# Reciprocal roots of a decoder trunk: from Newton steps on VectorE to a power on GpSimd

## The chip, the cores and the metric

The kernel runs on one core of a Trainium2 chip. The metric is the time of one execution on the device, in microseconds; lower is better. The core has five engines that run their own queues of instructions in order and meet at semaphores: TensorE (PE in the profile; its weight loads are PEld), VectorE (DVE), ScalarE (ACT), GpSimd (POOL) and SyncE (SP), which here only issues DMAs.

## The reference

Two layers work on a sequence of 2048 tokens of width 1024 in float32: a gated DeltaNet layer (GDN: 8 heads, keys of 128, values of 256) and a gated linear attention layer (GLA: 4 heads, the same sizes). Each ends in `x <- LayerNorm(alpha*x + mixer(x))`. What matters here are the places where a reciprocal root stands:

```python
def l2norm(t):
    return t * lax.rsqrt(jnp.sum(t * t, -1, keepdims=True) + L2_EPS)      # L2_EPS = 1e-6

def gated_rmsnorm(o, w, gate):
    o = o * lax.rsqrt(jnp.mean(o * o, -1, keepdims=True) + RMS_EPS)       # RMS_EPS = 1e-6
    return o * w.astype(jnp.float32) * jax.nn.silu(gate.astype(jnp.float32))

def layer_norm(x, g, b):
    xf = x.astype(jnp.float32)
    mu = jnp.mean(xf, -1, keepdims=True)
    xc = xf - mu
    var = jnp.mean(xc * xc, -1, keepdims=True)
    y = xc * lax.rsqrt(var + LN_EPS) * g.astype(jnp.float32) + b.astype(jnp.float32)   # LN_EPS = 1e-5
    return y.astype(x.dtype)

def gdn_mixer(x, w_in, conv_w, a_log, dt_bias, norm_w, w_out):
    ...
    q = l2norm(qkv[..., :GDN_KEY].reshape(B, T, GDN_HEADS, GDN_DK).astype(f32))
    k = l2norm(qkv[..., GDN_KEY:2 * GDN_KEY].reshape(B, T, GDN_HEADS, GDN_DK).astype(f32))
    ...
    o = gated_delta_rule(q, k, v, g, beta)
    o = gated_rmsnorm(o, norm_w, gate)
    return o.reshape(B, T, GDN_VAL).astype(x.dtype) @ w_out
```

The delta rule's output `o` is linear in `q`, so the norm of `q` is one factor for each token and head. GLA normalises its output in the same way, but neither `q` nor `k`.

## The kernel before

**Tiling.** The sequence is cut into 4 groups of 512 tokens (`TG`), each of 4 chunks of 128 (`NC`). A unit of work is one head of one layer on one group: 32 GDN units and 16 GLA units, in the order of `PHASES` (GDN of groups 0 and 1, then the layers in turn). Matrix products are done as three products of a high and a low part (`mm3`); the weights are loaded as `wraw`, ScalarE casts them to `wh`, and GpSimd subtracts to get `wl`. Nine such pairs of buffers exist (`W_BUFS`), and three PSUM tiles `psg` take the products.

**Four threads.** For each unit, `gemms` makes the input projection (`psg`), the short convolution (`acc`, on VectorE) and the gates (`sg`); `preps` makes what depends on keys and queries; `chains` runs the recurrence over the 4 chunks (`psh`, state `S`) and gathers the gated outputs `og` and their sums of squares `ssq`; `outs` multiplies by the output weights into `pso` and adds to `y`. `pso` has one buffer. The threads are interleaved by `Plan`: it prices every instruction as it is emitted (`COST`: a fixed time, a time for each element, and 800 ns until another instruction can use the result) and emits the next step whose operands it believes ready. The order of emission is the order of urgency; each engine then gets its own queue. Waits on semaphores follow from the tiles.

**The roots.** `rsqrt` works on VectorE: two operations on the bits make a first guess and nine operations (three steps of three) refine it. It is called in three places.

- In `gdn_prep`, once a unit: ScalarE squares the transposed keys and queries and accumulates their sums in `ss` (8 columns: 4 chunks of `k`, 4 of `q`); after the root `rr`, VectorE forms `rqs` (the root for `q`, scaled by 128 to the power of -0.5), `brk`, `br2` and `s1`. The products of keys (`D<-psc,br,D`) need `br2`. From there the preparation goes on: `W`, `X`, a transfer `blk` to memory and back as `Arep`, an inversion in 30 short steps of VectorE (`Xt`, `X`), and the matrices for `chains`. GpSimd takes part with a copy of `id16` into the buffer of `X`, which must wait until the transfer out of `X` has read it.
- In `chains`, once a unit: from `ssq` (and `rqs` for GDN) comes `z`, the factor for each token with which `outs` adds the product: `y <- pso * z + y`.
- In `layer_norm`, once for each chunk of 128 tokens of each layer, 32 times: `lnva` to `lnrs` and `lnmr`, which ScalarE then applies to `y`; VectorE multiplies by the gain, GpSimd adds the offset (VectorE in the very last chunk), and SyncE stores.

`load_wo` loads the output weights as `woraw`, and multiplies them by the norm's weight `nw` when it splits them (`woh` on ScalarE, `wol` on VectorE).

All engine operations but the DMAs' landings stand at one line of the profile, L121, since `Planned` issues them there; groups are told apart by their tiles. `z` is written by several operations, `ms`, `ztmp` beside it; `rr` goes with `rtmp`, `lnrs` with `lntmp`.

## Time and profile before

| what | value |
|---|---|
| median of 3 runs | 3253.21 us (3250.49 to 3254.4) |
| span of the profiled execution, first to last instruction | 3246.0 us |
| instructions | 55989 |
| traffic with memory | 91 GB/s over the span |

The profiled execution has no time of its own beside its span; the runs' median lies 7.2 us above it. The times in the profile are those of one execution. In the groups of instructions a line gives engine, operation, `out<-in` by the program's names, shapes and the count, then the busy time in us and the mean of one in ns, then the idle time of the engine just before them and what ended it. A line of waits gives who waited for whom, the total in us, how often, and the longest. A line of the timeline gives start and duration in us; `x4` are four in a row, and brackets hold the idle time before and its cause.

### The profile page before, as it was taken

What the parts mean: (1) busy time and instruction counts of PE and PEld (TensorE: products, weight loads), DVE (VectorE), ACT (ScalarE), POOL (GpSimd) and SP (SyncE); (2) the same over time, 40 slices, a digit from 0 to 9 for tenths busy, and PEclk for the clock granted to TensorE, in tenths of its full rate; (3) what the DMA queues carried; (4) which work ended last, traced back from release to release, by engine and by line L of the source; (5) the groups of instructions that cost most, each with busy time, mean ns of one, the idle gap of its engine ahead of it and who ended that gap; (6) DMA issues with size and microseconds to landing.
All of it is one profiled execution on the core that took longest, in us unless ns stands there. A gap on an engine that the chain in (4) does not pass through costs nothing.

```text
span 3246.0 us, 55989 instructions
## 1 busy us (share of the span) xinstructions
PE 3064.1 (94%) x18430; PEld 2601.6 (80%) x18430; DVE 2466.0 (76%) x6345; ACT 1565.6 (48%) x4099; POOL 1127.2 (35%) x1506
## 2 busy tenths in 40 slices
PE   8899999989999999998999999999899999899997
PEld 7688778768888888877887888978778878798885
DVE  7677788787877687688778768677877786866677
ACT  5445444445444456444444545553444454465542
POOL 5333333333233234334233324432433322433341
PEclk9899999999999999999999999999999999999998
DMA  6222223242222315324222322532422232243231
GB/s 179 63 77 74 78 73 98 82 147 76 74 78 78 101 53 153 109 79 127 80 79 82 92 73 67 153 98 78 136 77 74 82 94 69 78 137 97 66 125 59
DMA packets 311604, 299.83 MB, mean 92 GB/s; under 512 B 40544, under 2 KB 253792, under 8 KB 311312
## 3 DMA queue, kind: packets, MB, share of 16 engines
q1 hardware_dynamic: 285200, 278.42, 30.0%
q10 hardware_dynamic: 26112, 17.83, 1.9%
q8 instruction: 145, 2.38, 0.3%
q14 instruction: 147, 1.20, 0.1%
HBM read 269.86 MB, written 26.28 MB: 91 GB/s over the span
## 4 chain that ended last, share of the span: by engine, by line
PE 47%; DVE 20%; DMA 7%; issue 2%; ACT 2%; POOL 0%; SPq 0%; DVEq 0%; ACTq 0%; POOLq 0%
PE psg L121 24%; PE psc L121 10%; PE pso L121 10%; DMA Arep<-blk 5%; PE psh L121 4%; DVE X L121 3%; DVE D L121 2%; DVE y L121 2%; DVE acc L121 2%; DVE Xt L121 2%; DVE lntmp L121 1%; DMA blk<-X 1%; DVE z L121 1%; DVE lnrs L121 1%; DVE lnst L121 1%
## 5 line engine op out<-in xcount | busy, mean ns | idle before, releaser
L121 POOL TENSOR_TENSOR wl<-wraw,wh 128x256 fp32r<-128x256 f32 x1152 | 950.0, 843 | 1349.7 <-ACT wh L121 1207.9
L121 ACT CAST wh<-wraw 128x256 fp32r<-128x256 f32 x1152 | 444.6, 405 | 373.9 <-PE psg L121 229.2
L121 PE MATMUL psg<-wh,xh 128*128 128x256 f32 (+1 forms) x2048 | 609.5, 298 | 12.8 <-ACT acc L121 6.1
L121 PE MATMUL psg<-wl,xh 128*128 128x256 f32 (+1 forms) x2048 | 586.4, 286 | 2.7 <-POOL wl L121 2.5
L121 PE MATMUL psg<-wh,xl 128*128 128x256 f32 (+1 forms) x2048 | 585.7, 286 | 0.0
L121 PE MATMUL psg<-xh,wh 128*128 128x512 f32 x1280 | 525.6, 411 | 2.9 <-DVE vt L121 1.3
L121 PE MATMUL psg<-xl,wh 128*128 128x512 f32 x1280 | 518.8, 405 | 0.6 <-DVE xl L121 0.6
L121 PE MATMUL psg<-xh,wl 128*128 128x512 f32 x1280 | 514.8, 402 | 0.1
L121 PEld LDWEIGHTS psg<-wh,xh 128*128 128x128 f32 x2048 | 392.6, 192 | 30.4 <-ACT acc L121 6.9
L121 PEld LDWEIGHTS psg<-wl,xh 128*128 128x128 f32 x2048 | 393.3, 192 | 16.5 <-POOL wl L121 3.8
L121 PEld LDWEIGHTS psg<-wh,xl 128*128 128x128 f32 x2048 | 392.9, 192 | 1.0
L121 PE MATMUL pso<-woh,oth 128*128 128x512 f32 x736 | 326.3, 443 | 61.7 <-DVE y L121 55.7
L121 DVE SCALAR_TENSOR_TENSOR acc<-pb,taps,acc 128x512 f32<-128x512 f32 x384 | 330.1, 862 | 44.4 <-ACT acc L121 39.1
L121 DVE SCALAR_TENSOR_TENSOR y<-pso,z,y 128x512 f32<-128x512 f32 x368 | 273.6, 743 | 111.7 <-PE pso L121 109.2
L121 PE MATMUL pso<-woh,otl 128*128 128x512 f32 x736 | 304.8, 414 | 12.9 <-DVE otl L121 11.5
L121 PE MATMUL pso<-wol,oth 128*128 128x512 f32 x736 | 298.6, 406 | 0.0
L121 PEld LDWEIGHTS psg<-xh,wh 128*128 128x128 f32 x1280 | 243.9, 191 | 56.1 <-DVE sg L121 3.2
L121 PEld LDWEIGHTS psg<-xh,wl 128*128 128x128 f32 x1280 | 242.7, 190 | 54.7 <-POOL wl L121 1.0
L121 PEld LDWEIGHTS psg<-xl,wh 128*128 128x128 f32 x1280 | 243.4, 190 | 53.4 <-DVE xl L121 2.5
L121 ACT ACTIVATE junk<-psc 128x128 bf16<-128x128 f32 (+1 forms) x448 | 144.2, 322 | 185.4 <-PE psc L121 150.8
L121 PEld LDWEIGHTS pso<-woh,oth 128*128 128x128 f32 x736 | 140.2, 190 | 100.9 <-DVE y L121 72.0
L121 DVE TENSOR_TENSOR Xt<-Arep,X 128x60 f32<-128x60 f32 (+14 forms) x480 | 131.9, 275 | 84.7 <-DMA Arep<-blk 76.6
(192 smaller groups left out, 5459.0 us busy)
## 6 DMA issues: line engine op xcount, KB each, us to landing
wraw<-in_w_in SPq DMA_DIRECT2D x1152, 128.0 KB, 2.3
woraw<-in_w_out SPq DMA_DIRECT2D x192, 256.0 KB, 3.6
Arep<-blk SPq DMA_DIRECT2D x32, 512.0 KB
woraw<-in_xT SPq DMA_DIRECT2D x32, 256.0 KB, 3.2
y<-in_x SPq DMA_DIRECT2D x16, 512.0 KB, 4.3
Gb<-gcT ACTq DMA_DIRECT2D x32, 256.0 KB, 3.0
x<-y SPq DMA_DIRECT2D x32, 256.0 KB, 2.1
x2T<-th ACTq DMA_DIRECT2D x32, 256.0 KB, 4.4
```

The costliest lines, as they stand in the source:

```text
L121: ins = op(*args, **kw)
```

## The change

`rsqrt` becomes one or two operations on GpSimd: an addition of the epsilon, where there is one, and a power with the exponent -0.5, which stands in a tile `mhalf`. The norm of `q` is not taken as a root any more. Before, with `rqs` = (ss_q + 1e-6)^-0.5 * 128^-0.5, `z` was 0.5/ALPHA * rqs * (rqs^2 * ssq/256 + 1e-6)^-0.5. Now it is (ssq + qn)^-0.5 with `qn` = (ss_q + 1e-6) * 128 * 256 * 1e-6, and the constant 0.5 * 256^0.5 / ALPHA (`NORM`) is multiplied once into the norm's weights `nw` at setup, for both layers. In `gdn_prep` the root is then taken of 4 columns in place of 8. A comment of `Plan` is also gone.

```diff
+NORM = 0.5 * DV ** 0.5 / ALPHA
...
+    mhalf = T("mhalf", [P, NC])
...
         sync.dma_start(nws[0][:], nw1)
+        v.tensor_scalar(nws[0][:], nws[0][:], NORM, None, ALU.mult)
...
+        v.memset(mhalf[:], -0.5)
...
         sync.dma_start(nws[1][:], nw2)
+        v.tensor_scalar(nws[1][:], nws[1][:], NORM, None, ALU.mult)
...
-    def rsqrt(y, a, tmp):
-        yi = y.bitcast(I32)
-        v.tensor_scalar(yi, a.bitcast(I32), 1, None, ALU.logical_shift_right)
-        v.tensor_scalar(yi, yi, -1.0, float(0x5F3759DF), ALU.mult, ALU.add)
-        for _ in range(3):
-            v.tensor_tensor(tmp, y, y, ALU.mult)
-            v.scalar_tensor_tensor(tmp, tmp, -0.5, a, ALU.mult, ALU.mult)
-            v.scalar_tensor_tensor(y, tmp, 1.5, y, ALU.add, ALU.mult)
+    def rsqrt(y, a, eps):
+        if eps:
+            g.tensor_scalar(y, a, eps, None, ALU.add)
+        g.tensor_tensor(y, y if eps else a, mhalf[:, :y.shape[1]], ALU.pow)
...
-        ss, r, tmp = small("ss", 2 * NC), small("rr", 2 * NC), small("rtmp", 2 * NC)
+        ss, r, qn = small("ss", 2 * NC), small("rr", NC), small("qn", NC)
...
-        v.tensor_scalar(ss[:], ss[:], 1e-6, None, ALU.add)
-        rsqrt(r[:], ss[:], tmp[:])
-        rk = r[:, 0:NC]
-        rqs, brk, br2, s1 = (small(k, NC) for k in ("rqs", "brk", "br2", "s1"))
-        v.tensor_scalar(rqs[:], r[:, NC:], float(P) ** -0.5, None, ALU.mult)
+        rsqrt(r[:], ss[:, :NC], 1e-6)
+        rk = r[:]
+        brk, br2, s1 = (small(k, NC) for k in ("brk", "br2", "s1"))
+        v.tensor_scalar(qn[:], ss[:, NC:], 1e-6, P * DV * 1e-6, ALU.add, ALU.mult)
...
-            ms, z, tmp = small("ms", NC), small("z", NC), small("ztmp", NC)
+            z = small("z", NC)
             if u.kind == 1:
-                v.tensor_scalar(ms[:], ssq[:], 1.0 / DV, 1e-6, ALU.mult, ALU.add)
-                rsqrt(z[:], ms[:], tmp[:])
-                v.tensor_scalar(z[:], z[:], 0.5 / ALPHA, None, ALU.mult)
+                rsqrt(z[:], ssq[:], DV * 1e-6)
             else:
-                rqs = u.prep["rqs"][:]
-                v.tensor_tensor(ms[:], rqs, rqs, ALU.mult)
-                v.scalar_tensor_tensor(ms[:], ms[:], 1.0 / DV, ssq[:], ALU.mult, ALU.mult)
-                v.tensor_scalar(ms[:], ms[:], 1e-6, None, ALU.add)
-                rsqrt(z[:], ms[:], tmp[:])
-                v.scalar_tensor_tensor(z[:], z[:], 0.5 / ALPHA, rqs, ALU.mult, ALU.mult)
+                v.tensor_tensor(ssq[:], ssq[:], u.prep["qn"][:], ALU.add)
+                rsqrt(z[:], ssq[:], 0.0)
...
-        va, rs, tmp, mr = (small(k, 1, LN_BUFS) for k in ("lnva", "lnrs", "lntmp", "lnmr"))
+        rs, mr = (small(k, 1, LN_BUFS) for k in ("lnrs", "lnmr"))
...
-        v.tensor_scalar(va[:], mv[:, 1:2], 1e-5 / ALPHA ** 2, None, ALU.add)
-        rsqrt(rs[:], va[:], tmp[:])
+        rsqrt(rs[:], mv[:, 1:2], 1e-5 / ALPHA ** 2)
```

## The prediction

> **What bounds the kernel now.** I read the page first, then TensorE's waits, then the groups by tile, then the timeline at the places they named. Page, parts 1 and 4 (busy time; the chain that ended last):

> ```profile
> PE 3064.1 (94%) x18430; PEld 2601.6 (80%) x18430; DVE 2466.0 (76%) x6345; ACT 1565.6 (48%) x4099; POOL 1127.2 (35%) x1506
> ...
> PE 47%; DVE 20%; DMA 7%; issue 2%; ACT 2%; POOL 0%; SPq 0%; DVEq 0%; ACTq 0%; POOLq 0%
> ```

> TensorE sets the pace; it is idle 3246.0 - 3064.1 = 182 us. VectorE is the only other engine of weight on the chain (20%); GpSimd is not on it. So the change is worth what VectorE makes TensorE wait, plus stretches without matmuls. Waits of TensorE alone (total us, times, longest):

> ```profile
> PE pso L121 <- DVE y L121: 60.8, 36, 5.4
> ...
> PE psg L121 <- POOL wl L121: 2.5, 3, 1.7
> ...
> PE psc L121 <- DVE Tm L121: 0.4, 1, 0.4
> ```

> Twenty rows name DVE, from 60.8 down to 0.4; they add up to 127 us. Nearly half is `y`: `pso` has one buffer, and the next output product waits until VectorE has added the last to `y`. The longest of these waits, on VectorE and on TensorE:

> ```profile
> 708.92 0.71 DVE L121 SCALAR_TENSOR_TENSOR ztmp<-ztmp,ms 128x4 f32<-128x4 f32 x1
> ...
> 710.85 0.72 DVE L121 SCALAR_TENSOR_TENSOR z<-ztmp,z 128x4 f32<-128x4 f32 x1
> ...
> 713.11 0.74 DVE L121 SCALAR_TENSOR_TENSOR y<-pso,z,y 128x512 f32<-128x512 f32 x1
> ```

> ```profile
> 713.90 0.80 PE L121 MATMUL pso<-woh,oth 128*128 128x512 f32 x1 [5.39 <-DVE y L121]
> ```

> Newton operations stand in line ahead of the `y` that TensorE needs: the two shown hold the engine for 0.7 each, 1.4 of 5.4 us, a quarter. From the end of `y` (713.85) to the matmul is a crossing of 0.05.

> **What goes.** A root costs two seed operations and nine Newton operations, for 32 preparations, 48 `z` and 32 layer norms: 112 roots, 1,008 Newton operations. Windows over the whole span for the three temporaries, each of which stands in every Newton operation of its kind:

> ```profile
> 0.00:3246.00 3246.00, 89.33 (x432) 0.98 0.32 92
> 0.00:3246.00 3246.00, 48.61 (x288) 0.98 0.32 92
> 0.00:3246.00 3246.00, 69.17 (x288) 0.98 0.32 92
> ```

> (`ztmp`, `rtmp`, `lntmp`.) Together 207 us. Seeds, epsilons and scalings are 14 more groups with 480 operations; the costliest, the cheapest, and one that prices what is added:

> ```profile
> L121 DVE TENSOR_SCALAR z<-z 128x4 int32<-128x4 int32 x64 | 13.1, 205 | 0.8
> ...
> L121 DVE TENSOR_SCALAR ss<-ss 128x8 f32<-128x8 f32 x32 | 5.5, 173 | 3.0 <-ACT junk L121 3.0
> ...
> L121 DVE TENSOR_SCALAR ms<-ssq 128x4 f32<-128x4 f32 x16 | 2.8, 173 | 0.0
> ```

> All 14 add up to 94 us: 301 us and 1,488 instructions leave VectorE. **What comes on VectorE:** 32 `qn` and 32 additions to `ssq`, at the 173 ns of `ss`, 11 us, and three tiny operations at the start, which I cost at nothing beside the first weight loads. VectorE falls by 290 us, to 2176 (67%).

> **What comes on GpSimd:** 80 additions of epsilon and 112 powers. GpSimd's rows:

> ```profile
> L121 POOL TENSOR_TENSOR y<-y,woraw 128x512 f32<-128x512 f32 x62 | 95.6, 1553 | 186.9 <-DVE y L121 90.8 <-DVE lntmp L121 85.3 <-DVE lnrs L121 6.3
> L121 POOL COPY pb<-halo 128x3 f32<-128x3 f32 x128 | 45.4, 355 | 99.2 <-DVE X L121 57.3 <-DVE Xt L121 21.3 <-DVE acc L121 16.8
> ```

> An addition on four elements is nearest to the copy of three, 0.35 us: 28 us. No row has a power. From below it is such a copy, 0.35 us; from above nothing in the trace caps it, and I keep 5 us, three times the longest GpSimd row. I take 1 us, three times the copy, which is the row with the nearest shape: 112 us. GpSimd goes from 1127 to about 1267 us, 39%. GpSimd's waits hide the new queueing: the `X` copy of the preparations (row below) holds that queue for up to 20 us, and yet TensorE waits for `wl` 2.5 us in all, since nine weight buffers lie ahead of it. So the weight splits behind a waiting power cost nothing up to such a delay.

> ```profile
> POOL X L121 <- DMA blk<-X: 443.1, 26, 20.0
> ```

> **The port.** One term speaks against the change; the tail's timeline shows it:

> ```profile
> 3226.77 0.15 DVE L121 SCALAR_TENSOR_TENSOR lnrs<-lntmp,lnrs 128x1 f32<-128x1 f32 x1
> ...
> 3228.63 3.00 POOL L121 TENSOR_TENSOR y<-y,woraw 128x512 f32<-128x512 f32 x2 [75.57 <-DVE lntmp L121]
> 3229.20 1.22 DVE L121 SCALAR_TENSOR_TENSOR lnrs<-lntmp,lnrs 128x1 f32<-128x1 f32 x1
> ```

> A one-element VectorE operation takes 0.15 us alone and 1.22 us while GpSimd runs: it is held until GpSimd's instruction ends. So 140 us of new GpSimd time can hold VectorE. [...] VectorE is at work 67% of the time, and its largest group with two SBUF operands,

> ```profile
> L121 DVE SCALAR_TENSOR_TENSOR acc<-pb,taps,acc 128x512 f32<-128x512 f32 x384 | 330.1, 862 | 44.4 <-ACT acc L121 39.1
> ```

> holds 330 us, 10% of the span. Between these ends I take 40%: 56 us back. Net relief 290 - 56 = 234 us, 9.5% of VectorE's work.

> **What that is worth.** In proportion, 9.5% of the 127 us: 12 us. By the quarter seen in the longest wait: 32 us. A queue at 67% in place of 76% may be shorter by half: 64 us. I take 32, the share that a row shows.

> The latency of the roots in mid-kernel counts nothing. In a preparation:

> ```profile
> 876.48 0.16 DVE L121 TENSOR_SCALAR ss<-ss 128x8 f32<-128x8 f32 x1
> ...
> 880.94 0.15 DVE L121 TENSOR_TENSOR br<-brk,rr 128x4 f32<-128x4 f32 x1
> ```

> 4.6 us, which become about 2.3 (0.35 + 1, two crossings, at 0.2 taken wide, and three small operations of 0.15), while TensorE has weight products to do; without that cover 32 times 2.3 us would show, 74 us, which the range doesn't count on. `z` took from 890.37 until the first `y` could go:

> ```profile
> 890.37 0.15 DVE L121 SCALAR_TENSOR_TENSOR ms<-ms,ssq 128x4 f32<-128x4 f32 x1
> ...
> 898.88 0.75 DVE L121 SCALAR_TENSOR_TENSOR y<-pso,z,y 128x512 f32<-128x512 f32 x1
> ```

> These 8.5 us become some 2; that is part of the 32.

> **The tail.** After the last matmul VectorE sets the end (a window's busy time of TensorE, its weight loads, VectorE, ScalarE and GpSimd; then VectorE's and ScalarE's lines in the timeline):

> ```profile
> 3230.00:3246.00 16.00, 0.00 (x0) 0.00 (x0) 12.71 (x28) 2.93 (x4) 8.03 (x6) 0.50 0.34 131
> ```

> ```profile
> 3225.72 0.69 DVE L121 BATCH_NORM_STATS2 lnst<-y 128x6 f32<-128x512 f32 x1
> ...
> 3236.07 2.93 ACT L121 ACTIVATE y<-y,lnmr,lnrs 128x512 f32<-128x512 f32 x4 [6.25 <-DVE lnmr L121]
> ```

> The last statistics end at 3226.4, but the last two tiles' Newton steps, held by GpSimd's `y`, let ScalarE start only at 3236.1. With powers: aggregate 0.2, add 0.35, power 1, crossings and `lnmr` 0.6: 3228.6, and up to 1.5 more behind a GpSimd `y`. The 9.9 us behind stay. 7.5 - 1.5: 6 us less (4 to 9).

> **Sum.** 3246.0 - 32 - 6 = 3208 us of span. The median of the runs, 3253.2, lies 7.2 above the span: **3215 us**. Ends: 64 and 9 give 3180; 12 and 4 give 3237.

> **Rivals.**
> *A, the waits refill* (14%). TensorE is 94% busy, and its order is fixed; a `y` that comes sooner only lets it meet the next late thing, ScalarE's copies or the `Arep` transfer. For: the chain passes through DMA for 7%. Against: 127 us of 182 idle name VectorE. Only the tail is left: 3247.
> *B, a power of many us* (13%), slower. At x us each, powers hold VectorE 0.4 × 112x = 45x us; with the 11 us of the additions that eats the 290 freed from x = 6.2 on. The preparation gets slower than its 4.6 us from about x = 3.3, `z` than its 8.5 from about 7. At 8 us VectorE has 80 us more, by the same quarter-rule 11 us of waits, and each of 32 preparations comes 4.7 later; with a quarter exposed, 38 us; the tail loses 1: about 3303. For: no row prices it. Against: four elements a partition are few, and GpSimd's longest row, on 512, is 1.55.
> *C, a power behind the `X` copy* (5%). `z` waits in GpSimd's order for a transfer. The copy's row:

> ```profile
> 888.82 0.24 POOL L121 COPY X<-id 128x64 f32<-128x64 f32 x1 [19.18 <-DMA blk<-X]
> ```

> It went 1.5 us before `z` could start (890.37), so in the usual unit it costs nothing; it decides where the copy is put first and its transfer is late. If it turned in a third of 32 units for 5 us, TensorE would lose 50: 3265.
> *D, all 74 us of the preparations' latency count* (3%): 3141.

> **How the numbers follow.** Forecast 65%. What counts as no change is within 0.2%, 3247 to 3260, about what a measurement of this kernel can tell. A lies on that edge, half and half: faster 0.65 + 0.03 + 0.07 = 0.75; same 0.07; slower 0.18 (B and C). The range 3180 to 3266 holds the forecast, A and C, and leaves out B, D and what the forecast's own ends may miss. The order of emission also moves, since the planner's own prices of the steps change; neither sign is known, and the range has room for it.

> **What would show it.** VectorE near 2230 us busy with some 4,920 instructions; powers of about 1 us; `pso` waiting for `y` under 45 us; ScalarE's last start some 6 us sooner against the last matmul. It is wrong if powers last over 3 us, if TensorE waits for GpSimd's `wl` or for `D`, or if `acc` and `Xt` get longer.

## The result, and the profile after

The changed kernel takes 3352.67 us (median of 4 runs, 3346.82 to 3354.55) where the kernel before takes 3252.34: a ratio of 1.0300, with a 95% interval of 1.0282 to 1.0318. It is 100 us slower. The forecast was 3215 with a range to 3266, so it was wrong in its sign and in its range. The profiled execution has a span of 3350.7 us, 104.7 more than before. Page of the changed kernel, part 1 (line 122 of its profile is line 121 of before's):

```profile
PE 3088.0 (92%) x18430; PEld 2633.5 (79%) x18430; DVE 2270.1 (68%) x4924; ACT 1569.5 (47%) x4099; POOL 1250.8 (37%) x1698
```

VectorE lost 196 us of work and 1,421 instructions, GpSimd gained 124 us, much as forecast. Yet TensorE is idle for 3350.7 - 3088.0 = 262.7 us in place of 181.9, and busy 23.9 longer: together the 104.7. An engine was relieved, and the engine that it feeds waits longer. The waits of TensorE (total us, times, longest):

```profile
PE psh L122 <- DVE S L122: 99.3, 34, 6.2
PE psh L122 <- DVE Rt L122: 31.2, 14, 6.4
PE psc L122 <- DVE D L122: 17.2, 12, 4.9
PE pso L122 <- DVE y L122: 14.3, 17, 2.1
```

The same view of the kernel before had these for the recurrence (its `y` row stands in the prediction):

```profile
PE psh L121 <- DVE S L121: 9.8, 5, 3.1
...
PE psh L121 <- DVE Rt L121: 1.7, 4, 0.5
```

The wait for `y` did shrink, from 60.8 to 14.3, better than the 45 that was asked of it. In its place stand `S` and `Rt` of the recurrence, 11.5 us before and 130.5 now. All rows that name VectorE rose together from 127 to 206 us; the one for `D`, a sign named in the prediction, from 1.6 to 17.2. VectorE is less busy and later at the same time, so the question is what it waits for. Some of its waits, the changed kernel's first:

```profile
DVE Xt L122 <- DMA Arep<-blk: 125.9, 31, 6.7
...
DVE brk L122 <- POOL rr L122: 40.5, 31, 2.6
...
DVE lnmr L122 <- POOL lnrs L122: 35.7, 32, 3.8
```

```profile
DVE Xt L121 <- DMA Arep<-blk: 76.6, 32, 5.3
```

The first step of the inversion (`Xt`) waits 49 us longer for its transfer, and VectorE now stands 76 us for GpSimd's powers, one stop for nearly every preparation and every layer norm. Other waits have grown as much (`acc` for ScalarE from 39.1 to 84.0, `kd` for ScalarE from 46.1 to 89.8), and what matters is which of them TensorE feels. A place where it feels the first: VectorE's timeline of the changed kernel (start, duration, what; idle before in brackets), then TensorE's:

```profile
1708.70 0.22 DVE L122 TENSOR_TENSOR Xt<-Arep,X 128x60 f32<-128x60 f32 x1 [4.03 <-DMA Arep<-blk]
...
1713.87 0.19 DVE L122 TENSOR_TENSOR X<-X,Xt 128x32 f32<-128x32 f32 x1
1713.98 0.47 DVE L122 SCALAR_TENSOR_TENSOR S<-S,eg,psh 128x256 f32<-128x256 f32 x1
```

```profile
1707.48 0.59 PE L122 MATMUL psh<-wt,kd 128*128 128x256 f32 x2
...
1714.51 1.16 PE L122 MATMUL psh<-S,kq 128*128 128x256 f32 x2 [4.94 <-DVE S L122]
```

The product that `S` needs was issued at 1707.48. But VectorE's queue had the inversion ahead of `S`: it stood 4 us for `Arep`, then did 16 steps of the inversion, each of which needs the last, with an `sg` and a `y` between them, and got to `S` at 1713.98. TensorE stood 4.94 us. This is the rule and not one place: in 20 of the 34 waits for `S`, 88 of the 99 us, VectorE stood for `Arep` between the product that `S` needs and `S`. In 12 of the 20 at most three steps of the inversion lay between, so there the wait is that for the transfer. In the kernel before, none of the five waits for `S` has it; `S` was out of the way when VectorE came to the same wait:

```profile
888.85 0.48 DVE L121 SCALAR_TENSOR_TENSOR S<-S,eg,psh 128x256 f32<-128x256 f32 x1
...
895.89 0.50 DVE L121 TENSOR_TENSOR Xt<-Arep,X 128x60 f32<-128x60 f32 x1 [2.13 <-DMA Arep<-blk]
```

No dependency in the code puts `Xt` ahead of `S`; only the order of emission does. That gave the first theory: not the powers cost the time, but the order that `Plan` chose when the roots got shorter. Its rival: the powers themselves, by their queue, their latency or a hold of VectorE like the 1.22 us for 0.15 in the tail of before.

### The profile page after: what moved, and what is told of

It reads as the page before. It is cut to its first block, busy times and chain, and to the rows that moved or that the text cites. A ratio compares the mean times of both kernels' runs of the same rounds, so it can differ in the third digit from the quotient of the medians.

```text
span 3350.7 us, 54654 instructions
## 1 busy us (share of the span) xinstructions
PE 3088.0 (92%) x18430; PEld 2633.5 (79%) x18430; DVE 2270.1 (68%) x4924; ACT 1569.5 (47%) x4099; POOL 1250.8 (37%) x1698
## 3 DMA queue, kind: packets, MB, share of 16 engines
q14 instruction: 137, 1.12, 0.1%
## 4 chain that ended last, share of the span: by engine, by line
PE 62%; DVE 16%; DMA 11%; POOL 4%; issue 4%; ACT 3%; SPq 0%; POOLq 0%; ACTq 0%; DVEq 0%
PE psg L122 34%; PE psc L122 12%; PE pso L122 11%; DMA Arep<-blk 6%; PE psh L122 5%; DVE D L122 2%; DVE y L122 2%; DVE X L122 2%; DVE acc L122 2%; POOL wl L122 2%; DMA blk<-X 1%; DVE Xt L122 1%; DMA x2T<-th 1%; POOL rr L122 1%; POOL y L122 1%
## 5 line engine op out<-in xcount | busy, mean ns | idle before, releaser
L122 POOL TENSOR_TENSOR wl<-wraw,wh 128x256 fp32r<-128x256 f32 x1152 | 959.8, 849 | 1262.8 <-ACT wh L122 1222.0
L122 PE MATMUL psg<-wh,xh 128*128 128x256 f32 (+1 forms) x2048 | 624.9, 306 | 15.9 <-DVE sg L122 7.5
L122 PE MATMUL psg<-xh,wh 128*128 128x512 f32 x1280 | 532.5, 416 | 9.0 <-DVE vt L122 3.6
L122 DVE TENSOR_TENSOR Xt<-Arep,X 128x60 f32<-128x60 f32 (+14 forms) x480 | 105.4, 220 | 137.8 <-DMA Arep<-blk 125.9
L122 ACT ACTIVATE th<-psg 128x256 f32<-128x256 f32 (+1 forms) x256 | 108.7, 435 | 160.1 <-PE psg L122 117.6
```

The source lines that it names most:

```text
L122: ins = op(*args, **kw)
```

## The experiments

Ratios are to the kernel before on the same chip, with 95% intervals; its own median lay between 3243.79 and 3261.16 us from chip to chip, so ratios are compared, not times. A difference of ratios is turned into microseconds with 3252 us.

### The order and the instructions, each alone

`Plan` learns of an instruction through a note. An instruction issued through `nc` itself leaves none, so one version's instructions can run in the order that the notes of the other lead to. *powers_old_order* has the change's instructions and before's notes:

```diff
-        rsqrt(r[:], ss[:, :NC], 1e-6)
+        rsqrt(r[:], ss[:, :NC], 1e-6, nc.gpsimd)
...
+        plan.note("v", [ss8, ss8])
+        newton_notes(r8, ss8, tmp)
...
+        plan.note("v", [rqs, as_ghost(r[:], NC)])
```

and the same for `z` and the layer norm; `newton_notes` leaves the notes of two seeds and nine Newton steps. *newton_new_order* is the reverse: before's instructions on `nc.vector`, with the notes of one addition and one power. The orders are near, not equal: with the traces' lists of TensorE's 18,430 matmuls aligned, 385 of *powers_old_order* stand otherwise than in the kernel before, where 5,425 of the changed kernel do; *newton_new_order* differs from the changed kernel in 492.

> The changed kernel's instructions (powers on GpSimd), but the planner is told before's steps, prices and dependences for every root, so that the order of emission is nearly before's. If the order made the loss: below before, 3200 to 3245 us (my 3215), with TensorE's wait for S back near 10 us from 99. If GpSimd's powers themselves made it (their latency, VectorE's wait for them, the shared port): it stays at 3330 to 3360.

> The mirror: before's instructions (Newton steps on VectorE), but the planner is told the changed kernel's steps, so that the order is nearly the changed kernel's. If the order made the loss: 3320 to 3400 us, as slow as the changed kernel or slower, with TensorE waiting some 100 us for S. If the powers made it: 3245 to 3260.

Measured: powers in the old order 1.0031 (1.0019 to 1.0044), 3265 us and so between the two expected ranges, near the first; Newton steps in the new order 1.0275 (1.0257 to 1.0294). With the old order the change of instructions costs next to nothing on balance; the order takes nearly all. TensorE's waits of *newton_new_order*, which has not one power:

```profile
PE psh L121 <- DVE S L121: 66.9, 34, 4.1
PE psh L121 <- DVE Rt L121: 32.2, 16, 4.6
```

They are the two rows that grew in the changed kernel, `S` here by less (to 66.9, where some 100 were expected, against 99.3 there), and 49 of the 66.9 us again have the wait for `Arep` in front of `S`. And with the powers in the old order they are small again, while the `y` is back:

```profile
PE pso L122 <- DVE y L122: 56.4, 48, 4.1
PE psh L122 <- DVE S L122: 16.2, 11, 3.1
```

Why the order changes can be read in the code: `Plan` prices a VectorE operation at 110 ns and 800 more until its result can be used. Eleven dependent operations of a root are some 10 us to it, an addition and a power some 2. It takes `br2`, `z` and the layer norm for ready some 8 us earlier and draws forward what follows. On the chip two dependent operations of a root start some 0.2 us apart where nothing comes between (891.45, 891.65 and 891.86 for the two seeds and the first Newton operation of a `z` in the timeline of before): the prices were not right before either, but the order that they led to was better.

### Which place moves the order

Before's notes for the preparations alone (*old_order_prep_only*), for `z` alone (*old_order_z_only*), and for both, so that only the layer norm has the new ones (*old_order_prep_and_z*); the instructions are the change's in all three.

> The changed kernel; the planner is told before's steps for the roots of the preparations only (their products are believed ready some 10 us later). If the preparations that the planner draws forward made the loss: within 30 us of the run with the whole old order. If z or the layer norms made it: above 3320.

> The changed kernel; the planner is told before's steps for z only. If z's earlier output products made the loss: within 30 us of the run with the whole old order. If the preparations made it: above 3320.

> The changed kernel; the planner is told before's steps for the preparations and for z, and the changed steps for the layer norms alone. If the loss lies in preparations and z moving against each other: within 15 us of the run with the whole old order (3265). If the layer norms' part counts: 3290 to 3325.

Measured: 1.0218 (1.0199 to 1.0236), 1.0316 (1.0299 to 1.0333) and 1.0054 (1.0035 to 1.0072). From the changed kernel's 1.0300 the preparations' notes give back 0.8%, those of `z` nothing, both together 2.5%. The effects don't add up, and by what was expected each of the first two runs puts the loss in the other place: the order has to be right in both. The layer norm's notes are worth some 0.2%.

### A yield ahead of the inversion

In `gdn_prep` there is no yield between the issue of the transfer and the first step that needs it, so the inversion goes into VectorE's queue whether the transfer has landed or not. One line lets `Plan` put other work there; it goes into the changed kernel (*changed_inversion_yields*) and into the powers in the old order (*old_order_inversion_yields*):

```diff
         R = T("Arep", [P, 16, NC, 16])
         sync.dma_start(R[:].rearrange("p s n j -> p (s n j)"),
...
+        yield ready(R)
         X = T("X", [P, NC, 16])
```

> The changed kernel with one line more: before the inversion the preparation gives way until the planner believes Arep landed, so that recurrence steps emitted meanwhile stand ahead of Xt in VectorE's queue. If Xt, waiting for Arep ahead of S, makes the loss: TensorE's wait for S from 99 to under 40 us and the time 3260 to 3300. If not: within 20 us of 3352.

> The run with powers and the old order, with the same line. There S waits 16 us in all, so if the line only cures Xt ahead of S it brings little: 3245 to 3270. If the planner's order there is also short of this: under 3240, better than both kernels.

Measured: 1.0172 (1.0155 to 1.0189) and 0.9933 (0.9913 to 0.9953). The second beats both kernels, 3240.48 us where before took 3261.16 on that chip. TensorE's waits of *changed_inversion_yields*:

```profile
PE pso L122 <- DVE y L122: 51.0, 34, 4.7
PE psh L122 <- DVE S L122: 36.1, 31, 3.7
PE psc L122 <- DVE og L122: 29.9, 16, 5.5
```

The wait for `S` fell by 63 us, as expected, and of what is left only 8 us have the wait for `Arep` in front of `S`, where it was 88: the inversion was the cause of most of that row. But the time fell by 1.3%, some 42 us, to 3318 where 3260 to 3300 was expected; `y` rose from 14.3 to 51.0 and `og` from 4.1 to 29.9 us. This mechanism is shown, then, and what its removal gave is less than half of the 87 us that the order costs. The line moves other work too, and the rest lies in the order elsewhere, which was not taken apart and stays open.

### What the relief of VectorE is worth, and what the powers give back

To see what the roots cost at all, each was replaced by one VectorE operation that gives a constant, with before's notes (*roots_for_nothing_old_order*); this kernel leaves out the reciprocal roots and shows a time alone. *powers_aside_old_order* has the same, and GpSimd computes all the additions and powers too, into a tile that nobody reads:

```diff
-        g.tensor_tensor(y, y if eps else a, mhalf[:, :y.shape[1]], ALU.pow)
+        nc.vector.tensor_scalar(y, a, 0.0, 0.15 if eps == 1e-6 else 0.5, ALU.mult, ALU.add)
...
+        nc.gpsimd.tensor_tensor(side, side if eps else a, mhalf[:, :y.shape[1]], ALU.pow)
```

> The run with the old order, but each root is one VectorE operation that writes a constant (no reciprocal root is computed): neither Newton steps nor powers. It bounds what taking the roots away can bring. If my term holds (a quarter of TensorE's 127 us on VectorE, and the tail): 3205 to 3225 us. If the waits refill (rival A): 3240 to 3260. If the powers' own waits cost the old-order run its 10 us over before and more: 30 to 45 us below that run.

> As roots_for_nothing_old_order (constants in place of the roots, same order on TensorE and VectorE), but GpSimd computes every addition and power as well, of the same sums, into a tile that nobody reads. If the powers cost by holding GpSimd's queue and the shared port: 3250 to 3265. If they cost by the time for which VectorE and ScalarE wait for their results: 3218 to 3230.

Measured: 0.9872 (0.9855 to 0.9888) and 0.9904 (0.9889 to 0.9919). Both kernels have the same order on TensorE and on VectorE, matmul by matmul and operation by operation. The pages of the two, first the constants alone, then with the powers aside:

```profile
PE 3059.2 (95%) x18430; PEld 2606.8 (81%) x18430; DVE 2337.7 (73%) x5036; ACT 1568.7 (49%) x4099; POOL 1123.7 (35%) x1506
```

```profile
PE 3051.6 (95%) x18430; PEld 2602.6 (81%) x18430; DVE 2333.7 (72%) x5036; ACT 1568.9 (49%) x4099; POOL 1248.1 (39%) x1698
```

Without the roots the kernel is 1.28% faster: 42 us, near the forecast's 32 + 6. The powers as mere work on GpSimd, 124 us of it, take 0.3% back (10 us, with intervals that just miss each other), and VectorE's busy time does not rise. So powers that somebody waits for must cost the other 1.3% that lies between 0.9904 and 1.0031. Where, was asked by giving one place its powers and the other two constants:

> As roots_for_nothing_old_order, with real powers for the 32 preparations, constants for z and the layer norms. If the cost goes with the count of powers: 32/112 of some 48 us, 14, so 3230 to 3238. If the preparations carry it (VectorE's brk stands in line for the power): 3245 or more. If they are covered: 3220 to 3226.

> As roots_for_nothing_old_order, with real powers for the 48 z, constants elsewhere. By count: 48/112 of 48 us, 21, so 3236 to 3246. If z carries it (y stands behind z, and pso has one buffer): 3250 or more. If covered: 3220 to 3226.

> As roots_for_nothing_old_order, with real powers for the 32 layer norms, constants elsewhere. By count: 14 us, so 3230 to 3238. If the layer norms carry it (a chain of VectorE, GpSimd, VectorE, ScalarE, VectorE, GpSimd in which each waits in line): 3245 or more; at the tail alone some 4 us.

Measured: preparations 1.0019 (1.0008 to 1.0030), `z` 0.9873 (0.9849 to 0.9898), layer norm 0.9951 (0.9936 to 0.9966). Against the 0.9872 of constants the preparations' powers cost 1.5% (48 us), the layer norms' 0.8% (26 us), those of `z` nothing. These prices don't add up either: 74 us one by one, 52 (1.0031 against 0.9872) all together. TensorE's order is no rival here, since these three kernels have at most 157 of 18,430 matmuls at another place than the one with constants. VectorE's waits, that of the preparations where they have the powers, and that of the layer norms where these have:

```profile
DVE brk L122 <- POOL rr L225: 34.7, 31, 2.1
```

```profile
DVE lnmr L122 <- POOL lnrs L225: 32.9, 30, 3.1
```

VectorE stands for the power in nearly every preparation and layer norm; in the run with powers for `z` no row of its waits names the `z` of GpSimd. What stands behind the waiting instruction shows in the timelines of *powers_old_order*, GpSimd's, then VectorE's:

```profile
872.63 1.04 POOL L224 TENSOR_TENSOR rr<-rr,mhalf 128x4 f32<-128x4 f32 x1
```

```profile
872.26 0.35 DVE L122 TENSOR_SCALAR kd<-psc,gdec 128x128 f32<-128x128 f32 x1
873.70 0.16 DVE L122 TENSOR_TENSOR brk<-beta,rr 128x4 f32<-128x4 f32 x1 [1.09 <-POOL rr L224]
...
873.98 0.75 DVE L122 SCALAR_TENSOR_TENSOR y<-pso,z,y 128x512 f32<-128x512 f32 x1
```

VectorE stands 1.09 us at `brk`, and behind it in line stand `y` and, at 874.71, `Rt`, for both of which TensorE has rows of waits. In the kernel before, the Newton steps of this place had such work between them. Averaged over the 32 preparations of each trace, from the end of the last sum of the keys' squares to the first product `D` on VectorE it takes 7.9 us in the kernel before, 6.2 with constants, 7.1 with the powers in the old order and 4.2 in the changed kernel. So `D` does come sooner without Newton steps, and the power gives back 0.9 of 1.7 us, near the length of its stop, which moves all that is behind it too. But an earlier `D` alone is worth little: with the powers it comes 0.9 us sooner than in the kernel before and the kernel is no faster, and in the changed kernel it comes 3.7 us sooner and the kernel is 100 us slower.

### Is it the stop alone?

*vector_time_at_prep* keeps the constants and puts three multiplications of 128x128 in each preparation where the root was, so VectorE is held by work for as long as the power held it:

```diff
+            for _ in range(3):
+                d.scalar_tensor_tensor(aside[:], C(C_ID), a[:, 3:4], C(C_ONE), ALU.mult, ALU.mult)
```

*mixed_old_order* takes the power where it is free, for `z`, and Newton steps on VectorE for the preparations and the layer norms.

> As roots_for_nothing_old_order, with three operations of 128x128 on VectorE (some 1.1 us, results unused but for a constant) in each preparation between its sums and brk. If VectorE's time at that place is the price, busy or idle: 0.999 to 1.005 of before, as with the powers of the preparations alone (1.0019). If the price is the wait for another engine: 0.985 to 0.993.

> Powers for z only; Newton steps on VectorE for the preparations and the layer norms (the norm of q stays under the root of z); the order of emission as before. If VectorE's idle wait at brk is what the powers of the preparations cost: below before by some 20 us (z's Newton steps and q's roots are gone), 3225 to 3245. If Newton steps there cost as much as the powers did: 3250 to 3270.

Measured: 0.9936 (0.9910 to 0.9961) and 1.0042 (1.0028 to 1.0056). The group of the three multiplications (busy, then the mean in ns):

```profile
L227 DVE SCALAR_TENSOR_TENSOR aside<-cst,ss 128x128 f32<-128x128 f32 x96 | 36.8, 383 | 1.0
```

That is 1.15 us for each preparation, near the 1.09 of the power's stop, and it costs 0.64% (21 us) where the power costs 1.5%, between the two ranges that were expected. A held VectorE thus makes close to half of the preparations' loss. The other half stays open; 435 of TensorE's 18,430 matmuls stand otherwise in this kernel than in the one with constants, so the half is rough. The mixed kernel gains nothing: beside 0.9873 with the powers of `z` alone, Newton steps for the preparations and the layer norms cost 1.7%, no less than the powers there do; its order, too, is only near to theirs.

### Orders that did not help

The line that gained 1% on the powers in the old order was tried on the kernel before (*newton_inversion_yields*) and on the mixed one (*mixed_inversion_yields*), and in *powers_both_yield* a second `yield ready(r)` was put between the power and `brk`, so that `Plan` could fill the stop.

> The kernel before with that line alone, all Newton steps. 3225 to 3240 if the line is worth 25 us by itself; then the powers of the whole old-order run added nothing. 3250 to 3260 if it isn't.

> The same with the line that lets the preparation give way before the inversion. The line brought 25 us to the run with powers and the old order: 3205 to 3230 if it brings the same here, 3225 to 3245 if it only mended what the powers had broken.

> Powers everywhere, old order, giving way before the inversion and also between the preparation's power and brk, so that other work may stand ahead of brk in VectorE's queue. If the idle wait at brk is the cost: VectorE's idle before brk from 35 us to under 10 and the time 3205 to 3230. If brk stays where it is or moves the inversion late: 3235 to 3260.

Measured: 1.0079 (1.0055 to 1.0103), 1.0040 (1.0022 to 1.0057) and 1.0125 (1.0104 to 1.0146). The same line makes the kernel before slower, the mixed one neither way (1.0042 without it), and the second yield costs 1.9% beside the 0.9933 with the first alone, although `brk` then waits 25.6 us in place of the 29.8 with one yield. All three lie above every range that was expected. Each such edit moves work elsewhere too, and moves the time by 1 to 2% in either direction; what it moves was not taken apart.

### The order, without any root

Last, the constants with the notes of the change:

> The changed kernel with constants in place of the roots (no reciprocal root is computed), the order of emission as in the changed kernel. If the order costs its 90 us whatever the roots are: 1.012 to 1.022 of before (0.9872 with the old order). If most of the loss is the roots' waits within that order: under 1.003.

Measured: 1.0116 (1.0086 to 1.0146), against 0.9872 in the old order. The first of TensorE's waits:

```profile
PE psh L122 <- DVE S L122: 85.4, 31, 4.9
```

In this row, 73 of the 85 us have the wait for `Arep` in front of `S`. So the new order costs about the same with all three kinds of roots:

| ratio to the kernel before | before's order | the change's order | the order costs |
|---|---|---|---|
| Newton steps on VectorE | 1 | 1.0275 | 89 us |
| powers on GpSimd | 1.0031 | 1.0300 | 87 us |
| constants | 0.9872 | 1.0116 | 79 us |

The last column is the difference of the ratios times 3252 us. The loss needs neither a power nor a Newton step.

## Why the prediction was wrong

**The step that failed** is the last sentence of how the numbers follow: "The order of emission also moves, since the planner's own prices of the steps change; neither sign is known, and the range has room for it." The range had 51 us of room above the forecast; the order took 87. It was treated as noise around the sum, and it is the largest term of the change. Its sign could not be had from the profile, but its size was open: a term with no row has ends, and none were given.

**"The latency of the roots in mid-kernel counts nothing"** was right about the latency, since an earlier `D` brought no time, and left out another cost: VectorE, which takes its queue in order, now stops at the root's first user, 1.1 us in the preparations and about the same in the layer norms. The prediction asked what hides a longer power on GpSimd's queue (the weight splits), and not what stands behind the first reader on VectorE's. Powers that are waited for, 1.3%, and their mere work on GpSimd, 0.3%, are the 1.6% between 0.9872 and 1.0031, which eats the gain; that the stop is the whole of the 1.3% is not shown.

**What goes:** "301 us and 1,488 instructions leave VectorE", a net of 290. The count holds (4,924 instructions, forecast 4,920). The time does not, once the order is held fixed:

```profile
PE 3079.3 (94%) x18430; PEld 2614.8 (80%) x18430; DVE 2324.2 (71%) x4924; ACT 1566.7 (48%) x4099; POOL 1245.8 (38%) x1698
```

VectorE of *powers_old_order* fell by 142 us, from 2466.0. Short operations overlap with their neighbours: take the 1,488 operations out of before's own trace, and the time in which VectorE does anything falls by 173 us, not by 301 (the section on the hardware has rows). Less the 11 us that come and the 17 by which `acc` got longer, that is about the 142. That the changed kernel came out at 2270.1, near the forecast's 2230, goes with its order.

**What comes:** the sizes were right. The powers in the groups of the changed kernel:

```profile
L122 POOL TENSOR_TENSOR z<-ssq,mhalf 128x4 f32<-128x4 f32 x32 | 35.7, 1117 | 284.0 <-DVE ssq L122 192.6 <-ACT woh L122 32.2 <-DVE X L122 32.1
L122 POOL TENSOR_TENSOR rr<-rr,mhalf 128x4 f32<-128x4 f32 x32 | 33.2, 1038 | 2.7
...
L122 POOL TENSOR_TENSOR lnrs<-lnrs,mhalf 128x1 f32<-128x1 f32 x32 | 18.9, 591 | 2.5
```

1.04 to 1.12 us where 1 was taken, 0.59 for the layer norms, and GpSimd at 1250.8 us where 1267 was. Rival B, "a power of many us", falls. So does C: with the old order the powers of `z` cost no time (*power_z_only*), and in the changed kernel TensorE waits for GpSimd's `z` once, 0.7 us. D, where the latency of the preparations counts in full, falls with the 3.7 us by which `D` comes sooner in the changed kernel: 32 times that is 118 us, and none of it was gained.

**The port:** so the prediction and two expectations call the hold of VectorE while GpSimd works; through what GpSimd holds it no run shows. "Between these ends I take 40%: 56 us back" was the author's estimate, and no run shows the 40%. With 124 us of new work on GpSimd and nobody waiting for it, VectorE was not busier (2333.7 us, and 2337.7 without it), and the whole cost is 0.3% of the time, 10 us.

**What that is worth:** "I take 32, the share that a row shows". Together with the tail, 38 us forecast and 42 measured, for roots that cost nothing. The agreement is largely luck. The 32 were read from Newton steps that stand ahead of `y`, and without any root, in the old order, TensorE waits for `y` nearly as long as the 60.8 us of before:

```profile
PE pso L122 <- DVE y L122: 57.1, 42, 5.7
```

All waits for VectorE together fell from 127 to 110 us there: 17 where 32 was taken. Nor was the wait for `y` a sign of the whole: in the changed kernel it fell by 46 us while the kernel lost 100.

**Rival A,** the waits refill, is nearest to what happened, but its bound was wrong. It let the next late thing take back the gain and no more; TensorE's waits came back larger, since the order of work had changed with them.

**The tail** got 2.6 us shorter, not 6: from the end of the last matmul to the end of the span 21.8 us before and 19.2 after. ScalarE's last start came no sooner either, 12.6 us after the last matmul's end where it was 11.9. GpSimd's timeline at the end of the changed kernel:

```profile
3334.46 2.86 POOL L122 TENSOR_TENSOR y<-y,woraw 128x512 f32<-128x512 f32 x2 [2.12 <-DVE y L122]
3337.30 0.22 POOL L122 TENSOR_SCALAR lnrs<-lnmv 128x1 f32<-128x1 f32 x1
3337.60 0.57 POOL L122 TENSOR_TENSOR lnrs<-lnrs,mhalf 128x1 f32<-128x1 f32 x1
3340.22 2.86 POOL L122 TENSOR_TENSOR y<-y,woraw 128x512 f32<-128x512 f32 x2 [2.06 <-DVE y L122]
```

Each root stands behind two additions of the offset, 2.86 us, and the next layer norm waits for the root. The prediction allowed up to 1.5 us for that once; it comes three times.

## What to carry to other kernels

Where a planner emits the instructions, a change of instructions is two changes: run the new instructions in the old order and the old ones in the new order before you judge either, since the order may weigh more (here 87 us against 10). When an operation moves to another engine, don't ask only how long it takes there: find its first reader, and see what stands behind that reader in its queue. And a wait that is measured is not a sum that can be won: taking it away lets the next one show, which may be longer.

## What the runs showed of the hardware

**A long wait cost TensorE more than its length.** The mean granted clock was 0.983 in the profiled execution of before and is 0.969 in that of after. Windows of the changed kernel around the wait for `S` (span, busy us of TensorE, weight loads, VectorE, ScalarE and GpSimd, then the granted clock, DMA share and GB/s):

```profile
1709.50:1714.50 5.00, 0.06 (x1) 0.00 (x0) 4.62 (x17) 0.41 (x1) 1.36 (x2) 1.00 0.29 79
1714.50:1715.70 1.20, 1.19 (x4) 1.01 (x5) 1.06 (x7) 0.00 (x0) 0.00 (x0) 0.54 0.05 14
1715.70:1717.00 1.30, 1.30 (x8) 1.30 (x8) 1.16 (x7) 0.00 (x0) 0.00 (x0) 0.50 0.00 0
1717.00:1720.00 3.00, 3.00 (x17) 2.76 (x17) 2.38 (x7) 1.55 (x4) 1.84 (x2) 0.83 0.15 44
```

**Durations of short operations overlap.** From the timeline of before, two steps of different roots in the tail:

```profile
3224.85 0.15 DVE L121 SCALAR_TENSOR_TENSOR lnrs<-lntmp,lnrs 128x1 f32<-128x1 f32 x1
3224.91 0.15 DVE L121 SCALAR_TENSOR_TENSOR lntmp<-lntmp,lnva 128x1 f32<-128x1 f32 x1
```

They start 0.06 us apart and show 0.15 each: the sum of such durations is more than the time that the engine gives them, in before 301 us against 173. That is most of why 290 us of removed durations were 142 of busy time; that `acc` got longer in the old order (906 ns in place of 862 on average, 17 us in all) is another part. It is as long with constants and no power at all (903 ns), so the powers are not its cause; what is stays open.

**A power of four elements a partition took 1.04 us on GpSimd,** of one element 0.57 to 0.59, as the means of most groups have it; the highest is 1.54, of the 16 `z` of the GLA in *old_order_inversion_yields*. That is much for the size (before's copy of three elements took 0.35), and the work alone, 124 us with the additions, cost 10 us.

**GpSimd held VectorE with other work than the powers.** In before, 113 of the 1,488 VectorE operations of the roots lasted 0.5 us or more, where the median is 0.16, and each of the 113 ended 12 to 29 ns behind an operation of GpSimd: 100 behind a `wl`, 13 behind a `y`, three of these in the tail. The 112 powers of the changed kernel show no such hold: no VectorE operation ended in those 12 to 29 ns behind one of them, and 105 ran wholly within one. With the same order on TensorE and VectorE, 124 us more of GpSimd cost 10 us, and `acc` takes 904 ns with them and 903 without.
